# A hybrid decoder step: value products and query sums in fewer runs, products of the old states on GpSimd, small sample copies on ScalarE

## The chip, the cores and the metric

The kernel runs on one core of one Trainium2 chip. The metric is the device time of one execution in microseconds (us). Before the change, three runs took 1385.62, 1386.16 and 1386.54 us; the median is 1386.16. The engines are named as in the profile: PE is TensorE (matrix products; PEld its weight loads), DVE is VectorE, ACT is ScalarE, POOL is GpSimd, and SP issues most of the transfers.

## The reference

One layer of a hybrid decoder takes a prompt of 256 tokens and eight sample streams of one token each. The change touches the two mixers that run side by side: attention in a sliding window, and a state-space scan (SSD). What matters of the reference, cut:

```python
def swa_banded(q, k, v, sinks):          # prompt: chunks of 128, keys of the chunk and the one before
    logits = jnp.einsum('bnqkgd,bnskd->bnkgqs', qb, kk) * HEAD_DIM ** -0.5
    p = sink_softmax(logits, mask[None, :, None, None], sinks)
    o = jnp.einsum('bnkgqs,bnskd->bnqkgd', p, vv)
...
def ssd_scan(xs, dt, a, bm, cm, h0, chunk):
    la = jnp.cumsum(dt * a, axis=2)
    seg = la[:, :, :, None] - la[:, :, None, :]
    decay = jnp.exp(jnp.where(causal, seg, -jnp.inf))
    cb = jnp.einsum('bclgn,bcsgn->bclsg', cm, bm)
    y = jnp.einsum('bclsgh,bcsghp->bclghp', cb[..., None] * decay, xdt)
...
    y = y + jnp.einsum('bclgn,bcghpn->bclghp', cm, h_prev) * jnp.exp(la)[..., None]
...
def _layer(...):
    proj = rms_norm(x, w['g_mix']) @ w['w_in']
    q, k, v, z, xbc, dt_raw = jnp.split(proj, IN_SPLITS, axis=-1)
    q = rms_norm(q.reshape(b, t, N_HEADS, HEAD_DIM), w['q_norm_g'])
```

After that come the output projection, a cross-attention and a feed-forward part with a short convolution. For a sample token the scan has one step: its old state `h0` (32 heads of 64 by 128, for each of eight streams) is multiplied by C of that stream and summed over the 128 state entries; that is the product of the old states with C.

## The kernel before

Prompt and samples stand side by side as 264 columns. Every projection is cut into weight pieces of 128x1024 numbers. SP loads a piece into `wraw` (L83), ScalarE writes its high half `whi` (L89), VectorE the rest `wlo` (L90), each with four buffers. `mm3` makes three products of every 128x128 slice with the 264 columns: high by high (L104), high by low (L105), low by high (L106). A piece holds eight slices, so it feeds 24 products. `proj` runs them for a pair of output blocks and hands both to an `evac` function.

The order of the instructions on each engine isn't written by hand in the part that changes: the framework's scheduler builds it when the program is built, taking weights and evacuations first (`tc.high_priority`), and keeping each engine's program in that order. `tc.issue_after(x)` adds an order: what is written inside it stands behind x. Buffers and PSUM banks limit it too: there are three banks for "mm", two for "t", one each for "s", "x" and "y". So the small work of attention and scan stands between the large products of the input projection (to about 355 us of the span).

The small products use part of the array: a product with 64 output rows takes half of the columns, one with 32 rows a quarter, at an offset. Neighbouring products of that kind are called a run here.

- The log decays `la` are summed with the triangle `tri` (L479); L482 makes the same sums transposed, in 32 rows for each chunk, and `laT` goes to memory by SP for use in `ssd_prompt` (L810).
- `q_sums`: L620 sums the squares of the queries, eight products of 32 rows, for two halves d of four j.
- `attn_first(j)` handles the first chunk for j and j+1, `attn_prompt(j)` the second for one j: scores, softmax, four transposes (L283), a copy to `pt`, then four value products of 64 rows (L602 and L564), and a copy to `attn`.
- `conv_side` takes two convolution blocks: the evacuated `u` (a ring of four), a small copy of its sample columns to `cnew` (L746, 24 in all), and three steps on VectorE for each block (L750). `conv_sample` reads `cnew` (L757). `z_pair` makes the gates; L896 copies its sample columns to `zsam` (16).
- `ssd_prompt(g)` runs the scan for one group of heads; L830 has eight products of 64 rows a chunk; on GpSimd stand the sum of `xs` (L844) and the decay of `hp` (L851).
- `ssd_sample(g)` multiplies old states by C: GpSimd issues the loads of `cb` (one buffer, L870) and `h0` (three buffers, L873), VectorE multiplies 128x512 (L874) and sums (L875), 32 times.

Of the kernel before, what the change touches and what calls it, by code (L numbers as in the profile page):

```python
# [48 lines left out]
def hybrid_decoder_step_kernel(ctx: ExitStack, tc: tile.TileContext, I, O):  # L49
# [11 lines left out]
    def psum(tag):  # L61
        return ps.tile([128, 512], F32, tag=tag, name=tag, bufs=banks[tag])
# [415 lines left out]
    dtan2 = dtan.rearrange("p c h -> p (c h)")  # L478
    PE.matmul(p[:, 0:64], tri, dtan2, start=True, stop=True)  # L479
    PE.matmul(p[:, 64:128], ones, dtan2, start=True, stop=True)  # L480
    for c in range(2):
        PE.matmul(p[0:32, 128 + c * 128:256 + c * 128], dtan[:, c, :], tri, start=True, stop=True)  # L482
# [42 lines left out]
    def attn_prompt(j, rq, nrq, c):  # L525

        pp = j // 4
        nk = 128 * (c + 1)
# [39 lines left out]
    def attn_first(j):  # L568

# [26 lines left out]
            tr(p[:, i * 128:i * 128 + 128], e[:, i, :])  # L596
        pt = mp.tile([128, 4, 128], F32, tag="bc", name="pt", bufs=2)
        S.copy(out=pt, in_=p.rearrange("p (a q) -> p a q", q=128))
        o = psum("t")
        for i in range(4):  # L600
            h = i % 2
            PE.matmul(o[64 * h:64 * h + 64, 128 * (i // 2):128 * (i // 2) + 128], vn[:, 0, pp, 64 * h:64 * h + 64], pt[:, i, :], start=True, stop=True)  # L602
        S.copy(out=attn[:, j:j + 2, 0:128], in_=o[:, 0:256].rearrange("p (i q) -> p i q", i=2))


    qsq = [T3(apool, 4, tag="R", name=f"qsq{i}", bufs=4) for i in range(2)]
# [8 lines left out]

            S.activation(out=qsq[j // 4][:, j % 4, :TP], in_=qT[:, j, :TP], func=AF.Square)
    pq = psum("s")
    for d in range(2):
        for j in range(4):
            PE.matmul(pq[32 * j:32 * j + 32, 0:TP], nw[:, d, :], qsq[d][:, j, :TP], start=d == 0, stop=d == 1)  # L620
# [29 lines left out]
    def second_chunk(pp):  # L650
# [6 lines left out]
        for h, (hs, ho) in enumerate(halves):  # L657
# [2 lines left out]
            S.copy(out=hi, in_=x)  # L660
            V.tensor_tensor(out=qs[pp][ho, :, h, :], in0=x, in1=hi.bitcast(F32), op=ALU.subtract)

    for j in range(0, 8, 2):
        attn_first(j)
    for j in range(8):
        if j % 4 == 0:
            second_chunk(j // 4)
        d = 2 * (j // 4)
        attn_prompt(j, rqs[:, :, j % 4, d:d + 2], nrqs[:, :, j % 4, d:d + 2], 1)

    def attn_sample():

# [69 lines left out]
    def conv_side(b0, us, dst):  # L742
        c = mp.tile([128, 2, TP], F32, tag="c", name="c", bufs=2)
        for m, u in enumerate(us):
            bi = b0 + m
            V.tensor_copy(out=cnew[:, bi, :], in_=u[:, TP:])  # L746
            w = [cwh[:, i * 24 + bi:i * 24 + bi + 1] for i in range(4)]
            S.activation(out=c[:, m, :], in_=u[:, 0:TP], func=AF.Identity, scale=w[0], bias=cwh[:, 96 + bi:97 + bi])
            for i in range(1, 4):
                V.scalar_tensor_tensor(out=c[:, m, :], in0=u[:, i:i + TP], scalar=w[i], in1=c[:, m, :], op0=ALU.mult, op1=ALU.add)  # L750
        S.activation(out=dst, in_=c, func=AF.Tanh)
        V.scalar_tensor_tensor(out=dst, in0=dst, scalar=1.0, in1=c, op0=ALU.add, op1=ALU.mult)
# [113 lines left out]
    def ssd_sample(g):  # L866
        for q in range(2):
            rows = slice(4 * q, 4 * q + 4)
            cb = mp.tile([128, 4, 128], F32, tag="cb", name="cb", bufs=1)
            nc.gpsimd.dma_start(out=cb, in_=dram_bc[1][8 * g + 4 * q:8 * g + 4 * q + 4, :].partition_broadcast(128))  # L870
            for i in range(4):
                h0 = mp.tile([128, 4, 128], F32, tag="h0", name="h0", bufs=3)
                nc.gpsimd.dma_start(out=h0, in_=I["h0"][4 * g + i][:, rows, :])  # L873
                V.tensor_tensor(out=h0, in0=h0, in1=cb, op=ALU.mult)  # L874
                V.tensor_reduce(out=ych[:, 4 * g + i, rows], in_=h0, op=ALU.add, axis=AX.X)  # L875

    def conv_group(g):
# [711 lines left out]
```

## Time and profile before

| what | value |
|---|---|
| median of three runs | 1386.16 us |
| the profiled execution | 1386.54 us |
| its span | 1384.3 us |
| L90, `wlo` on DVE | 440 times, 540.7 us |
| L89, `whi` on ACT | 440 times, 459.5 us |
| L874, old states by C, DVE | 32 times, 22.5 us |
| L875, their sums, DVE | 32 times, 21.3 us |
| L746 and L896, small copies, DVE | 24 and 16 times, 3.9 and 2.4 us |
| L564 / L602, value products, records of PE | 64 / 32 |
| L620, query sums, records of PE | 16 |

A product in full precision leaves two records on PE, so a run of eight products shows 16. The span is what the profiler saw between the first and the last instruction; the time of an execution holds 2.24 us more in this one. In a row, a name such as `t<-xh,wlo` is the output tile and the inputs, and the bracket or the arrow behind an idle time names what ended it.

### The profile page before, as it was taken

Reading aid. Unit: us, or ns where it says so; the run is one execution under the profiler, and the core shown is the slowest. Engines: PE = TensorE matmul, PEld = TensorE weight load, DVE = VectorE, ACT = ScalarE, POOL = GpSimd, SP = SyncE. Lnnn points to the kernel's source line nnn. Section 1 sums busy time; section 2 is a strip of 40 time slices with the busy share of each in tenths; the row PEclk is TensorE's granted clock in tenths of the full one; section 3 lists DMA queues with packets and bytes.
Section 4 is the critical chain, followed back from the end, with each engine's and each line's share of the span. In section 5 each row is a group of like instructions: output and inputs, shape, how many; then the busy total and the mean of one; then the engine's idle time right before and its main releaser. Section 6 shows DMA issues by size and latency. Waiting matters only on the chain.

```text
span 1384.3 us, 28768 instructions
## 1 busy us (share of the span) xinstructions
PE 1376.5 (99%) x11415; PEld 1348.3 (97%) x11415; DVE 1048.7 (76%) x1865; ACT 766.1 (55%) x1261; POOL 94.8 (7%) x286
## 2 busy tenths in 40 slices
PE   9999999999999999999999999999999999999999
PEld 8999999999999999889999999999999999999998
DVE  7979799999987774478777775777577757765655
ACT  7667755556545555476565544554455445543532
POOL 0000011111000000002010000000000000000000
PEclk9999999999999999999999999999999999999999
DMA  7954467777677566766576765676667656655664
GB/s 296 331 163 135 145 209 254 232 245 259 234 220 239 182 240 211 308 219 193 187 256 216 259 210 188 214 255 214 186 214 244 196 185 198 198 183 185 192 188 139
DMA packets 89477, 298.31 MB, mean 215 GB/s; under 512 B 12032, under 2 KB 17152, under 8 KB 88832
## 3 DMA queue, kind: packets, MB, share of 16 engines
q1 hardware_dynamic: 83840, 277.61, 60.6%
q0 software_dynamic: 5504, 18.88, 4.2%
q8 instruction: 89, 1.46, 0.4%
q14 instruction: 44, 0.36, 0.1%
HBM read 280.77 MB, written 16.23 MB: 215 GB/s over the span
## 4 chain that ended last, share of the span: by engine, by line
PE 97%; DMA 1%; DVE 1%; ACT 0%; issue 0%; SPq 0%; ACTq 0%
PE mm L105 21%; PE mm L104 20%; PE mm L106 20%; PE t L105 10%; PE t L106 9%; PE t L104 9%; PE t L245 1%; PE t L283 1%; PE y L830 1%; DMA wraw<-in_w_co_dram 1%; PE y L846 0%; DMA open<-in_open_dram 0%; PE x L283 0%; DVE wlo L90 0%; PE s L245 0%; PE mm L245 0%
## 5 line engine op out<-in xcount | busy, mean ns | idle before, releaser
L89 ACT CAST whi<-wraw 128x1024 fp32r<-128x1024 f32 x440 | 459.5, 1047 | 518.2 <-PE mm L105 278.3
L90 DVE TENSOR_TENSOR wlo<-wraw,whi 128x1024 fp32r<-128x1024 f32 x440 | 540.7, 1231 | 220.8 <-ACT whi L89 214.9
L105 PE MATMUL t<-x2l,whi 128*128 128x264 f32 x704 | 200.6, 285 | 0.0
L105 PE MATMUL mm<-x2l,whi 128*128 128x264 f32 x704 | 200.5, 285 | 0.0
L105 PE MATMUL mm<-hl,whi 128*128 128x264 f32 x704 | 199.6, 285 | 0.0
L106 PE MATMUL t<-x2h,wlo 128*128 128x264 f32 x704 | 199.1, 283 | 0.0
L106 PE MATMUL mm<-x2h,wlo 128*128 128x264 f32 x704 | 198.7, 283 | 0.0
L106 PE MATMUL mm<-hh,wlo 128*128 128x264 f32 x704 | 197.6, 282 | 0.0
L104 PE MATMUL mm<-x2h,whi 128*128 128x264 f32 x704 | 196.5, 279 | 0.4 <-DVE res L1285 0.4
L104 PE MATMUL t<-x2h,whi 128*128 128x264 f32 x704 | 196.4, 279 | 0.0
L104 PE MATMUL mm<-hh,whi 128*128 128x264 f32 x704 | 194.1, 280 | 0.0
L104 PE MATMUL mm<-xh,whi 128*128 128x264 f32 x576 | 163.8, 286 | 0.0
L105 PE MATMUL mm<-xl,whi 128*128 128x264 f32 x576 | 163.5, 285 | 0.0
L106 PE MATMUL mm<-xh,wlo 128*128 128x264 f32 x576 | 162.1, 286 | 0.0
L104 PEld LDWEIGHTS mm<-x2h,whi 128*128 128x128 f32 x704 | 132.3, 188 | 0.6 <-ACT whi L89 0.6
L104 PEld LDWEIGHTS t<-x2h,whi 128*128 128x128 f32 x704 | 132.3, 188 | 0.0
L106 PEld LDWEIGHTS t<-x2h,wlo 128*128 128x128 f32 x704 | 132.1, 188 | 0.0
L106 PEld LDWEIGHTS mm<-x2h,wlo 128*128 128x128 f32 x704 | 132.1, 188 | 0.0
L106 PEld LDWEIGHTS mm<-hh,wlo 128*128 128x128 f32 x704 | 131.9, 188 | 0.0
L105 PEld LDWEIGHTS mm<-hl,whi 128*128 128x128 f32 x704 | 131.7, 187 | 0.0
L105 PEld LDWEIGHTS mm<-x2l,whi 128*128 128x128 f32 x704 | 131.7, 187 | 0.0
L105 PEld LDWEIGHTS t<-x2l,whi 128*128 128x128 f32 x704 | 131.7, 187 | 0.0
(497 smaller groups left out, 2893.8 us busy)
## 6 DMA issues: line engine op xcount, KB each, us to landing
wraw<-in_w_up_dram SPq DMA_DIRECT2D x176, 512.0 KB, 4.4
wraw<-in_w_in_dram SPq DMA_DIRECT2D x96, 512.0 KB, 4.7
wraw<-in_w_dn_dram SPq DMA_DIRECT2D x88, 512.0 KB, 4.4
wraw<-in_w_out_dram SPq DMA_DIRECT2D x48, 512.0 KB, 4.3
h<-in_h_dram POOLq DMA_DIRECT2D x32, 256.0 KB, 4.6
hn<-in_h_dram SPq DMA_DIRECT2D x16, 512.0 KB, 4.8
out_state_s_dram<-hn POOLq DMA_DIRECT2D x16, 512.0 KB, 3.6
e<-dram_la SPq DMA_DIRECT2D x16, 256.0 KB, 4.8
```

Of the source, the lines that this page charges most:

```text
L89: S.copy(out=hi, in_=x)
L90: V.tensor_tensor(out=lo, in0=x, in1=hi.bitcast(F32), op=ALU.subtract)
L104: PE.matmul(out, wh, xh, start=start, stop=False)
L105: PE.matmul(out, wh, xl, start=False, stop=False)
L106: return PE.matmul(out, wl, xh, start=False, stop=stop)
L245: PE.matmul(first[c][:, :T], pre[k // 2][i][:, k % 2, c * 128:(c + 1) * 128], A[k // 8][x][:, k % 8, :], start=k + i + x == 0, stop=k == K ...
L283: return PE.transpose(out, in_, cst[0:k, C_ID:C_ID + k])
L830: PE.matmul(y[o:o + 64, (h // 2) * 128:(h // 2) * 128 + 128], xdt[:, h, :], es[h // 4][:, h % 4, :], start=True, stop=True)
```

## The change

It has five parts. The transposed log decays are no longer summed by L482 but made by one transpose of `la` (64 rows, both chunks at once). The query sums begin with d=1, j=3, the last to be ready, and the other seven stand behind it by `issue_after`. The value products are taken out of the two attention functions, and two calls share one run of eight, which begins with the first product of the later call. The small copies of sample columns go from VectorE to ScalarE. The product of old states with C goes from VectorE to GpSimd, and its sum stays on VectorE.

```diff
-    for c in range(2):
-        PE.matmul(p[0:32, 128 + c * 128:256 + c * 128], dtan[:, c, :], tri, start=True, stop=True)
...
-    laT = next_u()[0:32, 3:259]
-    V.tensor_copy(out=laT, in_=p[0:32, 128:384])
-    nc.sync.dma_start(out=dram_la.rearrange("c h l -> h c l"), in_=laT.rearrange("p (c l) -> p c l", c=2))
+    laT = next_u()[0:64, 3:131]
+    p = psum("x")
+    tr(p[0:64, 0:128], la)
+    V.tensor_copy(out=laT, in_=p[0:64, 0:128])
+    nc.sync.dma_start(out=dram_la.rearrange("c h l -> (c h) l"), in_=laT)
...
-        pt = mp.tile([128, 4, 128], F32, tag="bc", name="pt", bufs=2)
+        pt = mp.tile([128, 4, 128], F32, tag=tag, name="pt", bufs=2 if tag == "bc" else 1)
         S.copy(out=pt[:, 0:2 * nb, :], in_=p[:, 0:2 * nk].rearrange("p (a q) -> p a q", q=128))
+        return pt
+
+    def second_values(j, pts):
+        pp = j // 4
         o = psum("t")
-        for h in range(2):
-            for kb in range(nb):
-                PE.matmul(o[64 * h:64 * h + 64, 0:128], vn[:, kb, pp, 64 * h:64 * h + 64], pt[:, h * nb + kb, :],
-                          start=kb == 0, stop=kb == nb - 1)
-        marks["attn"] = S.copy(out=attn[:, j, c * 128:c * 128 + 128], in_=o[:, 0:128])
+
+        def value(a, h, kb):
+            return PE.matmul(o[64 * h:64 * h + 64, 128 * a:128 * a + 128], vn[:, kb, pp, 64 * h:64 * h + 64], pts[a][:, 2 * h + kb, :],
+                             start=kb == 0, stop=kb == 1)
+
+        with tc.issue_after(value(1, 0, 0).ins):
+            for x in [(a, h, kb) for a in (1, 0) for h in range(2) for kb in range(2)][1:]:
+                value(*x)
+        marks["attn"] = S.copy(out=attn[:, j:j + 2, 128:TP], in_=o[:, 0:256].rearrange("p (i q) -> p i q", i=2))
...
+    def first_values(pp, pts):
...
+        with tc.issue_after(value(1, 0).ins):
+            for a, i in [(a, i) for a in (1, 0) for i in range(4)][1:]:
+                value(a, i)
+        S.copy(out=attn[:, 4 * pp:4 * pp + 4, 0:128], in_=o.rearrange("p (i q) -> p i q", i=4))
...
-    for d in range(2):
-        for j in range(4):
-            PE.matmul(pq[32 * j:32 * j + 32, 0:TP], nw[:, d, :], qsq[d][:, j, :TP], start=d == 0, stop=d == 1)
+    with tc.issue_after(q_sums(1, 3).ins):
+        for d in (1, 0):
+            for j in range(4):
+                if (d, j) != (1, 3):
+                    q_sums(d, j)
...
+    for pp in range(2):
+        first_values(pp, [attn_first(4 * pp + 2 * a) for a in range(2)])
...
+        second_values(j, [attn_prompt(x, rqs[:, :, x % 4, d:d + 2], nrqs[:, :, x % 4, d:d + 2], 1, tag)
+                          for x, tag in zip((j, j + 1), ("bc", "bc") if j % 4 == 0 else ("hp", "cb"))])
...
-            V.tensor_copy(out=cnew[:, bi, :], in_=u[:, TP:])
+            S.copy(out=cnew[:, bi, :], in_=u[:, TP:])
...
-                V.tensor_tensor(out=h0, in0=h0, in1=cb, op=ALU.mult)
+                P.tensor_tensor(out=h0, in0=h0, in1=cb, op=ALU.mult)
...
-            V.tensor_copy(out=zsam[:, 2 * i + m, :], in_=z[:, TP:])
+            S.copy(out=zsam[:, 2 * i + m, :], in_=z[:, TP:])
```

The lines of the changed program lie lower down: the query sums are L637, the second values L568, the first L615, the conv steps L774, the scan's products L854, the products of old states L898 and their sums L899.

Three places show how the order moves. The first is PE at the query sums, in the input projection. Before, the eight products stand in three runs:

```order
L106 MATMUL mm<-xh_77,wlo 128x264
L620 MATMUL s<-qsq_677,zz 32x256 x4
L620 MATMUL s<-qsq_678,zz 32x256 x2
L104 MATMUL mm<-xh_75,whi 128x264
...
L105 MATMUL mm<-xl_76,whi 128x264
L620 MATMUL s<-qsq_678,zz 32x256
L106 MATMUL mm<-xh_75,wlo 128x264
```

Now, with the transpose of `la` one large product ahead of them:

```order
L104 MATMUL mm<-xh_75,whi 128x264
L283 MATMUL x<-cst,la 64x128
L105 MATMUL mm<-xl_76,whi 128x264
L637 MATMUL s<-qsq_678,zz 32x256 x4
L637 MATMUL s<-qsq_677,zz 32x256 x4
L106 MATMUL mm<-xh_75,wlo 128x264
```

All eight stand together now, the half that is ready last first (`qsq_678`). The second place is PE at the value products of the second chunk (`vn` are the values). Before, four of them, next to transposes of the following probabilities `pe`:

```order
L106 MATMUL mm<-xh_77,wlo 128x264
L564 MATMUL t<-pt,vn 64x128 x4
L283 MATMUL t<-cst,pe 128x128 x4
L283 MATMUL x<-cst,bcs 32x128
L104 MATMUL mm<-xh_77,whi 128x264
```

Now:

```order
L105 MATMUL mm<-xl_78,whi 128x264
L106 MATMUL mm<-xh_77,wlo 128x264
L568 MATMUL t<-pt,vn 64x128 x8
L283 MATMUL x<-cst,bcs 32x128
L104 MATMUL mm<-xh_77,whi 128x264
```

The products of two calls stand in one run, and the transposes ahead of it. The third place is DVE at the second half of the old states of one group. Before, products and sums of `h` stand between the weight pieces and the scan:

```order
L90 TENSOR_TENSOR wlo<-wraw,whi 128x1024
L874 TENSOR_TENSOR h_3147<-h_3147,cb 128x512
L874 TENSOR_TENSOR h_3151<-h_3151,cb 128x512
L90 TENSOR_TENSOR wlo<-wraw,whi 128x1024
L739 TENSOR_TENSOR u_655<-mm,r_423 128x264
L752 SCALAR_TENSOR_TENSOR xs_2164<-xs_2164,c 128x2x256
L875 TENSOR_REDUCE ych<-h_3147 128x4
```

Now there are only the sums on DVE:

```order
L90 TENSOR_TENSOR wlo<-wraw,whi 128x1024
L899 TENSOR_REDUCE ych<-h_3135 128x4
L776 SCALAR_TENSOR_TENSOR xs_2152<-xs_2152,c 128x2x256
L899 TENSOR_REDUCE ych<-h_3139 128x4
L90 TENSOR_TENSOR wlo<-wraw,whi 128x1024
L899 TENSOR_REDUCE ych<-h_3143 128x4
```

The products of the same three tiles stand on POOL, between the issues of the loads:

```order
L894 DMA cb<-dram_bc 128x512
L897 DMA h_3143<-in_h_dram 128x512
L898 TENSOR_TENSOR h_3135<-h_3135,cb 128x512
L898 TENSOR_TENSOR h_3139<-h_3139,cb 128x512
L898 TENSOR_TENSOR h_3143<-h_3143,cb 128x512
L897 DMA h_3147<-in_h_dram 128x512
```

Each sum on DVE now stands behind a product on another engine, and the load of the next tile behind three products.

More of the change, by code (lines that the diff above doesn't have):

```diff
@@ L523, in hybrid_decoder_step_kernel, with attn_prompt @@
     V.tensor_scalar(out=nsink, in0=pc("sink_p", 0, 16), scalar1=-1.0, scalar2=None, op0=ALU.mult)
-    def attn_prompt(j, rq, nrq, c):
+    def attn_prompt(j, rq, nrq, c, tag):
         pp = j // 4
@@ L598, in attn_first, with value @@
         S.copy(out=pt, in_=p.rearrange("p (a q) -> p a q", q=128))
+        return pt
+    def first_values(pp, pts):
         o = psum("t")
-        for i in range(4):
+        def value(a, i):
             h = i % 2
-            PE.matmul(o[64 * h:64 * h + 64, 128 * (i // 2):128 * (i // 2) + 128], vn[:, 0, pp, 64 * h:64 * h + 64], pt[:, i, :], start=True, stop=True)
-        S.copy(out=attn[:, j:j + 2, 0:128], in_=o[:, 0:256].rearrange("p (i q) -> p i q", i=2))
+            c = 256 * a + 128 * (i // 2)
+            return PE.matmul(o[64 * h:64 * h + 64, c:c + 128], vn[:, 0, pp, 64 * h:64 * h + 64], pts[a][:, i, :], start=True, stop=True)
+        with tc.issue_after(value(1, 0).ins):
+            for a, i in [(a, i) for a in (1, 0) for i in range(4)][1:]:
+                value(a, i)
+        S.copy(out=attn[:, 4 * pp:4 * pp + 4, 0:128], in_=o.rearrange("p (i q) -> p i q", i=4))
     qsq = [T3(apool, 4, tag="R", name=f"qsq{i}", bufs=4) for i in range(2)]
@@ L617, in hybrid_decoder_step_kernel, with q_sums @@
     pq = psum("s")
-    for d in range(2):
-        for j in range(4):
-            PE.matmul(pq[32 * j:32 * j + 32, 0:TP], nw[:, d, :], qsq[d][:, j, :TP], start=d == 0, stop=d == 1)
+    def q_sums(d, j):
+        return PE.matmul(pq[32 * j:32 * j + 32, 0:TP], nw[:, d, :], qsq[d][:, j, :TP], start=d == 1, stop=d == 0)
+    with tc.issue_after(q_sums(1, 3).ins):
[3 more added lines that the diff above has]
+                    q_sums(d, j)
     cpc = mp.tile([128, 24, 8], F32, name="cpc")
@@ L661, in second_chunk @@
             V.tensor_tensor(out=qs[pp][ho, :, h, :], in0=x, in1=hi.bitcast(F32), op=ALU.subtract)
+    for pp in range(2):
+        first_values(pp, [attn_first(4 * pp + 2 * a) for a in range(2)])
     for j in range(0, 8, 2):
-        attn_first(j)
-    for j in range(8):
         if j % 4 == 0:
@@ L668, in hybrid_decoder_step_kernel @@
         d = 2 * (j // 4)
-        attn_prompt(j, rqs[:, :, j % 4, d:d + 2], nrqs[:, :, j % 4, d:d + 2], 1)
+        second_values(j, [attn_prompt(x, rqs[:, :, x % 4, d:d + 2], nrqs[:, :, x % 4, d:d + 2], 1, tag)
+                          for x, tag in zip((j, j + 1), ("bc", "bc") if j % 4 == 0 else ("hp", "cb"))])
     def attn_sample():
```

## The prediction

> **What bounds the kernel now.** I read the page first, from the top.
>
> ```profile
> span 1384.3 us, 28768 instructions
> PE 1376.5 (99%) x11415; PEld 1348.3 (97%) x11415; DVE 1048.7 (76%) x1865; ACT 766.1 (55%) x1261; POOL 94.8 (7%) x286
> PE 97%; DMA 1%; DVE 1%; ACT 0%; issue 0%; SPq 0%; ACTq 0%
> ```
>
> TensorE (PE) is busy for 99% of the span, and the third line, the chain that ended last, lies on it for 97%. So the time is the sum of what TensorE is given plus its few waits. The view of waits gives total, count and longest in us:
>
> ```profile
> PE x L206 <- DVE eps L279: 1.2, 1, 1.2
> ```
>
> That is the longest of six such rows with TensorE waiting, 4.4 us in all, and none between 31 and 580 us, where the change lies. A saving can come only from shorter work on TensorE, and a loss only from a wait that is new. What could be late is the low half of a weight piece, which VectorE (DVE) writes at L90. The next view has one stretch a row: its length, then busy us and count on PE, PEld, DVE, ACT and POOL, the granted clock, the DMA share and GB/s. The first two rows are of L90 alone, the next two of L106 alone, the last of everything.
>
> ```profile
> 0.00:185.30 185.30, 54.64 (x45) 1.00 0.62 209
> 0.00:294.10 294.10, 93.98 (x77) 1.00 0.68 222
> 0.00:191.40 191.40, 100.08 (x353) 65.91 (x353) 1.00 0.63 211
> 0.00:296.60 296.60, 170.14 (x609) 112.88 (x609) 1.00 0.68 222
> 185.30:294.10 108.80, 108.80 (x941) 105.71 (x940) 107.47 (x214) 60.72 (x103) 19.14 (x28) 1.00 0.77 242
> ```
>
> The 45th piece's low half is there at 185.3 us; L106 uses eight slices a piece, so its 353rd product, at 191.4, is the first that needs it: a lead of 6.1 us. The 77th is ready at 294.1 and needed at 296.6: 2.5 us. Between the two VectorE is busy for 107.5 of 108.8 us; it loses 3.6 us against TensorE. Here it is the second bound, close behind. The clock is 1.00 in all rows, so no term comes from it.
>
> **The change: TensorE.** A timeline row is the start, the duration, then engine, line, operation and count. Starts of the products after a run give its price.
>
> ```profile
> 355.80 0.28 PE L106 MATMUL t<-xh,wlo 128*128 128x264 f32 x1
> 355.92 0.28 PE L104 MATMUL t<-xh,whi 128*128 128x264 f32 x1
> 356.13 1.09 PE L830 MATMUL y<-e,xdt 128*64 128x128 f32 x16
> ...
> 357.38 0.28 PE L104 MATMUL t<-xh,whi 128*128 128x264 f32 x1
> 369.64 0.28 PE L105 MATMUL mm<-atl,whi 128*128 128x264 f32 x1
> 369.85 0.66 PE L830 MATMUL y<-e,xdt 128*64 128x128 f32 x8
> ...
> 370.67 0.28 PE L105 MATMUL t<-atl,whi 128*128 128x264 f32 x1
> ```
>
> A large product takes a slot of 0.12 us (355.80 to 355.92). The run of 16 records, eight products on half the columns, takes 1.46 from 355.92 to 357.38, less two slots 1.22. The run of 8 records takes 1.03, less two slots 0.79. So two runs of four products made into one of eight save 2 x 0.79 - 1.22 = 0.36: entering and leaving the column mode costs that much. The first values lose two runs (4 to 2, 0.72), the second ones four (8 to 4, 1.44; I take 1.4, since some stand beside transposes), and one run at L830 goes as the order falls (0.36): 2.5 us.
>
> ```profile
> 79.58 0.33 PE L479 MATMUL x<-dtan,cst 128*128 128x64 f32 x2
> 79.75 0.39 PE L480 MATMUL x<-dtan,cst 128*128 128x64 f32 x2
> 80.07 0.62 PE L482 MATMUL x<-cst,dtan 128*32 128x128 f32 x4
> ...
> 80.85 0.29 PE L106 MATMUL mm<-xh,wlo 128*128 128x264 f32 x1
> 81.22 0.28 PE L106 MATMUL mm<-xh,wlo 128*128 128x264 f32 x1
> 81.43 1.06 PE L620 MATMUL s<-qsq,zz 128*32 128x256 f32 x12
> 82.64 0.29 PE L105 MATMUL mm<-xl,whi 128*128 128x264 f32 x1
> 83.37 0.28 PE L105 MATMUL mm<-xl,whi 128*128 128x264 f32 x1
> 83.58 0.62 PE L620 MATMUL s<-qsq,zz 128*32 128x256 f32 x2
> ...
> 84.35 0.29 PE L104 MATMUL mm<-xh,whi 128*128 128x264 f32 x1
> ```
>
> Query sums: the run of 12 takes 1.42 less two slots, 1.18; that of 2 takes 0.98 less two, 0.74, and the third, alike, 0.74: 2.66 in all. One run of 16 lies above 1.18 and below 1.66, if the four added records cost no more than the 0.24 by pairs that starts at full width show; the middle, 1.42, saves 1.24 (1.0 to 1.48). Log decays: 79.75 to 80.85, 1.10, holds L480, the strip run and L105. Afterwards there is L480 at 0.17 (as from 79.58 to 79.75), one slot, and a transpose between one slot and 0.23: 0.41 to 0.52, so 0.6 is saved (0.58 to 0.69). Together 2.5 + 1.2 + 0.6 = **4.3 us** off TensorE (3.8 to 4.8). Nothing hides these: the chain runs through them.
>
> **The change: VectorE and GpSimd.** These rows group a line's instructions: count, busy us, mean ns, idle time before; the DVE rows between 185.3 and 294.1 us, the two POOL rows over the whole span. Then come timeline rows, the last from behind that stretch.
>
> ```profile
> L750 DVE SCALAR_TENSOR_TENSOR c<-u,par,c 128x256 f32<-128x256 f32 x38 | 18.7, 502 | 0.0
> L874 DVE TENSOR_TENSOR h<-h,cb 128x512 f32<-128x512 f32 x20 | 13.4, 681 | 0.9 <-DMA h<-in_h_dram 0.9
> L875 DVE TENSOR_REDUCE ych<-h 128x4 f32<-128x512 f32 x19 | 12.7, 676 | 0.0
> L746 DVE COPY cnew<-u 128x11 f32<-128x11 f32 x12 | 2.0, 164 | 0.0
> ...
> L844 POOL TENSOR_TENSOR xs<-xs,ti 128x512 f32<-128x512 f32 x4 | 9.1, 2264 | 2.5 <-DVE ti L843 2.4
> L851 POOL TENSOR_TENSOR hp<-hp,d 128x512 f32<-128x512 f32 x4 | 5.5, 1363 | 20.9 <-PE y L838 8.8 <-ACT xs L751 6.1 <-DMA wraw<-in_w_in_dram 5.9
> 239.83 1.04 POOL L851 TENSOR_TENSOR hp<-hp,d 128x512 f32<-128x512 f32 x1
> ...
> 240.26 1.69 DVE L90 TENSOR_TENSOR wlo<-wraw,whi 128x1024 fp32r<-128x1024 f32 x1 [0.32 <-ACT whi L89]
> ...
> 247.14 3.27 POOL L844 TENSOR_TENSOR xs<-xs,ti 128x512 f32<-128x512 f32 x1
> ...
> 249.20 1.50 DVE L750 SCALAR_TENSOR_TENSOR c<-u,par,c 128x256 f32<-128x256 f32 x1
> ...
> 290.39 1.31 POOL L851 TENSOR_TENSOR hp<-hp,d 128x512 f32<-128x512 f32 x1 [6.11 <-ACT xs L751]
> 290.72 1.26 DVE L875 TENSOR_REDUCE ych<-h 128x4 f32<-128x512 f32 x2
> 291.91 0.67 DVE L874 TENSOR_TENSOR h<-h,cb 128x512 f32<-128x512 f32 x1
> ...
> 342.00 2.37 DVE L874 TENSOR_TENSOR h<-h,cb 128x512 f32<-128x512 f32 x2
> ```
>
> A start-to-start distance for the 128x512 operations is 0.60 us (1.19 for the two reduces from 290.72 to 291.91). Between the 45th and the 77th low half VectorE now does 20 products (12.0 us) and 14 small copies (1.0 by the same distances, 0.075 each). Both go. But the order of the changed program has 30 reduces there for 19 (6.6 us more), and other work that it moves ahead, conv steps and parts of ssd_prompt, for 7.0 more. So the work in the stretch comes to 106.8 against 106.2 us by one set of prices: the relief is spent in the same stretch. TensorE's own share of moved small products makes its stretch longer too, 107.7 after 105.2 (191.4 to 296.6).
>
> What is new is contention. At 249.20 a conv step of mean 502 ns took 1.50 behind a GpSimd sum that ran from 247.14: about 1.0 us lost. The two reduces at 290.72 ran beside a GpSimd product at their usual 0.60. The products on GpSimd have no row; the nearest, L851 of the same size, takes 1.04 at best, against the 0.60 saved. I read the time lost on VectorE beside each of the eight GpSimd operations of ssd_prompt in that way (0.46 at 240.26, where L90 took 1.69 for its mean of 1.23; 1.09 at 342.00, where two products took 2.37 for 1.28): 0, 0, 0.19, 0.26, 0.31, 0.46, 1.02 and 1.09, 3.3 us beside 14.6 us of GpSimd (9.1 and 5.5), 0.23 a microsecond. A product of 1.04 at that rate costs 0.24. The changed order has more reduces near, and the share of VectorE's work with two operands in SBUF falls from about 66 to 57%, which makes x = **0.2 us** a product; the ends are 0 and 1.09.
>
> The first low half that VectorE can't give in time sets the stall. With 30 products and four operations of ssd_prompt in the stretch it is 34x + 0.9 (waits for DMA, as now) + 106.8 - 107.7 - 6.1 = **34x - 6.1**. At x = 0.2 that is 0.7 us.
>
> The Trainium skill ("SBUF — State Buffer", section "Who interferes with whom") speaks against this part: a VectorE instruction with two SBUF inputs and a GpSimd instruction that reads SBUF exclude each other for a whole instruction, while a reduce is never held. The trace agrees on the reduce (290.72) and on the one long hold (249.20); that two of eight operations cost nothing says that not every one meets such an instruction.
>
> The small copies on ScalarE cost nothing as long as it has room: it is busy for 60.7 of 108.8 us in the stretch, and 14 copies there would be 2.3 us at L746's 164 ns. If that cover goes, csm waits on VectorE for a copy, about 0.2 a block of four, eight blocks, 1.6 at most. On GpSimd's queue the products stand between the issues of the h0 and cb loads, so one that waits for its load or for cb holds the next load, and the hp and xs operations of ssd_prompt behind it; VectorE meets that only at L899 (rival 3). The pt copies that borrow the hp and cb buffers do so before the first cb load, which they could only delay. On SP's queue the write of la keeps its place, and one weight load now goes ahead of the first read of it, so no load comes later.
>
> **The sum.** The profiled execution took 1386.54, 2.24 outside the span; the sum is against the median, 1386.16, 0.38 below. 1386.16 - 4.3 + 0.7 = **1382.6**.
>
> **Rivals.** (1) *The holds eat the gain.* With x from 0.22 to 0.39 the stall is 1.4 to 7.2 us, and the net lies within about 0.2% (2.8 us, about what a measurement of this kernel can tell from no change). At x = 0.31 the stall is 4.4: 1386.3. For it: four of the eight values lie at 0.19 to 0.46. Against: those include operations longer than 1.04. Chance 0.26. (2) *The holds cost more than the runs save.* The place is the same stretch, the price x above 0.39; it ends slower. At the plain mean of the eight, 0.42, the stall is 8.2 and the time 1390.1; at 1.04 for each product, 29.3 and 1411. For it: two of eight reached 1.0, and VectorE hardly pauses, so a GpSimd operation nearly always meets something. Against: 18 us of reduces and the operations that read PSUM. Chance 0.21. By the skill's rule taken literally the 1411 would be the time. (3) *VectorE waits for GpSimd at the reduces.* L899 stands in VectorE's order; the next low half queues behind it. With 30 reduces each late by 0.3, on top of x = 0.2, the stall is 9.7: 1391.6. Chance 0.06; products are issued well ahead in the new order, with three buffers. (4) *The runs don't get cheaper*, since the value products of a pair now wait for the later pt on TensorE: 0.4 us at each of six runs takes 2.4 of the 4.3, which gives 1386.16 - 1.9 + 0.7 = 1385.0. No wait stands there now. Chance 0.05.
>
> **Numbers.** Faster 0.42 (the forecast), same 0.31 (1 and 4), slower 0.27 (2 and 3). The forecast's own range is 1381.0 to 1383.4. The whole range: below, 4.8 saved with no stall, 1381.4, and 0.4 for a sum read too small; above x = 0.53, stall 11.9, 1393.8, with the rest of the figures' rounding 1394.0. Higher x is left out, some 1 in 10.
>
> **What would show it.** Right: one run of 16 records at L637 of about 1.4 us, six value runs of 16 at 1.2, no TensorE wait for wlo between 185 and 310 us, conv steps with a mean near 0.5, L898 near 1.1. Wrong: rows "PE <- DVE wlo L90" in that stretch, L90 and L774 with means well above 1229 and 502 ns, or idle time of VectorE before L899 put down to GpSimd.

## The result and the profile after

The changed kernel takes 1401.56 us, the median of four runs (1400.66 to 1403.67), beside 1386.33 for the kernel before in the same comparison. The ratio is 1.0113, with a 95% interval of 1.0101 to 1.0125: 15.2 us slower. The forecast was 1382.6, with a range up to 1394.0.

The page of the changed kernel, its span, busy times and the chain that ended last:

```profile
span 1399.9 us, 28747 instructions
PE 1378.4 (98%) x11412; PEld 1350.8 (96%) x11412; DVE 1049.9 (75%) x1793; ACT 769.3 (55%) x1295; POOL 141.6 (10%) x318
PE 90%; DVE 3%; DMA 3%; POOL 2%; issue 1%; ACT 0%; SPq 0%; POOLq 0%; DVEq 0%
```

TensorE's idle time rose from 7.8 to 21.5 us, and its busy time from 1376.5 to 1378.4, although it has less to do. VectorE is as busy over the whole program as before (1049.9 for 1048.7): 32 products and 40 copies left it, and it has nothing to show for it. The waits of the changed kernel between 175 and 420 us (total, count, longest):

```profile
PE y L870 <- DVE ti L867: 3.9, 2, 3.5
DVE ych L899 <- POOL h L898: 3.5, 3, 2.2
PE mm L104 <- DVE u L763: 3.4, 2, 2.1
PE t L106 <- DVE wlo L90: 2.1, 2, 1.8
```

TensorE now waits for evacuations, for a low half and for parts of the scan, nearly all from VectorE (1.2 us are for ScalarE, in rows not shown), and VectorE waits for GpSimd at the sums. Groups of the same stretch show where VectorE's time went (count, busy us, mean ns, idle before):

```profile
L90 DVE TENSOR_TENSOR wlo<-wraw,whi 128x1024 fp32r<-128x1024 f32 x70 | 91.3, 1305 | 10.9 <-ACT whi L89 10.7
L774 DVE SCALAR_TENSOR_TENSOR c<-u,par,c 128x256 f32<-128x256 f32 x42 | 29.1, 710 | 0.0
L899 DVE TENSOR_REDUCE ych<-h 128x4 f32<-128x512 f32 x32 | 21.5, 673 | 3.5 <-POOL h L898 3.5
L898 POOL TENSOR_TENSOR h<-h,cb 128x512 f32<-128x512 f32 x32 | 51.1, 1603 | 45.5 <-DMA cb<-dram_bc 22.7 <-DMA h<-in_h_dram 22.5
```

A conv step costs 710 ns where it cost about 500, a weight piece 1305 where it cost 1229, and a sum what it always cost. On the timeline one sees it happen:

```profile
218.82 2.06 POOL L898 TENSOR_TENSOR h<-h,cb 128x512 f32<-128x512 f32 x1 [1.71 <-DMA h<-in_h_dram]
219.66 1.51 DVE L774 SCALAR_TENSOR_TENSOR c<-u,par,c 128x256 f32<-128x256 f32 x1
221.09 0.67 DVE L840 TENSOR_TENSOR e<-e,s 128x512 f32<-128x512 f32 x1
221.43 1.29 POOL L898 TENSOR_TENSOR h<-h,cb 128x512 f32<-128x512 f32 x1
221.69 1.09 DVE L785 SCALAR_TENSOR_TENSOR ysam<-tsm,csm 128x32 f32<-128x32 f32 x1
222.70 0.67 DVE L899 TENSOR_REDUCE ych<-h 128x4 f32<-128x512 f32 x1
```

The conv step at 219.66 has its two operands in SBUF and takes 1.51 beside the product at 218.82. L840, whose second operand is in PSUM, takes its usual 0.67 beside the next product. The tiny gate product at 221.69, with two operands in SBUF again, lasts until that GpSimd product is over. This is called a hold below. Its size for a whole kernel is the sum, over VectorE's instructions between 175 and 440 us, of what each takes beyond the usual duration of its form (the median over the kernel before and the one with the runs alone). In this kernel all instructions lengthened by more than 0.06 us stand beside GpSimd operations with two inputs.

### The profile page after: what moved, and what is told of

It reads as the page before. It is cut to its first block, busy times and chain, and to the rows that moved or that the text cites. A ratio compares the mean times of both kernels' runs of the same rounds, so it can differ in the third digit from the quotient of the medians.

```text
span 1399.9 us, 28747 instructions
## 1 busy us (share of the span) xinstructions
PE 1378.4 (98%) x11412; PEld 1350.8 (96%) x11412; DVE 1049.9 (75%) x1793; ACT 769.3 (55%) x1295; POOL 141.6 (10%) x318
## 4 chain that ended last, share of the span: by engine, by line
PE 90%; DVE 3%; DMA 3%; POOL 2%; issue 1%; ACT 0%; SPq 0%; POOLq 0%; DVEq 0%
PE mm L104 19%; PE mm L106 19%; PE mm L105 19%; PE t L104 9%; PE t L106 9%; PE t L105 9%; POOL h L898 1%; DMA h<-in_h_dram 1%; DMA cb<-dram_bc 1%; DVE c L774 1%; PE t L245 1%; DVE wlo L90 1%; PE t L283 1%; PE mm L245 0%; PE s L245 0%
## 5 line engine op out<-in xcount | busy, mean ns | idle before, releaser
L90 DVE TENSOR_TENSOR wlo<-wraw,whi 128x1024 fp32r<-128x1024 f32 x440 | 545.7, 1242 | 232.3 <-ACT whi L89 226.2
L106 PE MATMUL t<-x2h,wlo 128*128 128x264 f32 x704 | 198.5, 282 | 0.0
L106 PE MATMUL mm<-x2h,wlo 128*128 128x264 f32 x704 | 198.2, 282 | 0.0
L106 PE MATMUL mm<-hh,wlo 128*128 128x264 f32 x704 | 197.2, 282 | 0.0
L106 PE MATMUL mm<-xh,wlo 128*128 128x264 f32 x576 | 164.8, 288 | 0.0
L106 PEld LDWEIGHTS t<-x2h,wlo 128*128 128x128 f32 x704 | 131.9, 187 | 0.0
L106 PEld LDWEIGHTS mm<-x2h,wlo 128*128 128x128 f32 x704 | 131.8, 187 | 0.0
L106 PEld LDWEIGHTS mm<-hh,wlo 128*128 128x128 f32 x704 | 131.7, 187 | 0.0
```

Of the source, the lines that this page charges most:

```text
L90: V.tensor_tensor(out=lo, in0=x, in1=hi.bitcast(F32), op=ALU.subtract)
L106: return PE.matmul(out, wl, xh, start=False, stop=stop)
```

## The experiments

All times are medians. In the table, the 40th and the 110th piece are the starts of the first product (L106) with the low half of that weight piece, read from windows that count L106 (313 and 873 products); the holds are summed as said, with the number of GpSimd operations of two inputs in that stretch. Eight of those belong to the scan and are in every kernel. The runs of the kernel before beside these lie between 1386.0 and 1386.4.

| kernel | us | 40th piece | 110th piece | holds, us |
|---|---|---|---|---|
| before | 1386.2 | 175.3 | 404.8 | 3.3 of 8 |
| the change | 1401.6 | 171.4 | 420.7 | 24.1 of 40 |
| e1, products back on VectorE | 1385.2 | 171.8 | 404.0 | 4.6 of 8 |
| e2, runs alone | 1385.4 | 169.7 | 404.3 | 5.2 of 8 |
| e3, products on GpSimd alone | 1408.7 | 174.9 | 426.5 | 26.2 of 40 |
| e4, copies on ScalarE alone | 1391.7 | 174.6 | 410.2 | 6.7 of 8 |
| e5, zeros for products, cb unread | 1397.7 | 171.6 | 418.2 | 3.4 of 8 |
| e6, sum ahead of product | 1403.5 | 171.4 | 421.6 | 28.4 of 40 |
| f1, zeros for products, cb read | 1398.2 | 171.0 | 416.1 | 4.1 of 8 |
| f4, sum ahead, and zeros | 1394.4 | 170.5 | 412.2 | 4.4 of 8 |
| f6, one product in four on GpSimd | 1387.1 | 171.6 | 405.0 | 10.8 of 16 |
| f2, runs, no products | 1383.8 | 169.5 | 402.5 | 4.3 of 8 |
| f3, before, no products | 1387.2 | 174.5 | 404.7 | 6.2 of 8 |
| e9, half the sums on ScalarE | 1385.0 | 171.0 | 403.9 | 4.4 of 8 |
| f5, e9 with the copies on ScalarE | 1387.4 | 170.9 | 406.1 | 5.9 of 8 |
| e10, all sums on ScalarE | 1389.6 | 169.8 | 408.0 | 5.2 of 8 |
| g1, the change with tiles spread | 1393.4 | 171.1 | 411.4 | 22.2 of 40 |
| g2, g1 with products on VectorE | 1388.7 | 170.9 | 400.8 | 3.9 of 8 |

The framework orders each of these programs anew, so an edit is never alone: it also moves what stands around it.

### The parts of the change

In the changed kernel, e1 puts the products back; e2 also the small copies. In the kernel before, e3 moves only the products, e4 only the copies.

```diff
 e1  -                P.tensor_tensor(out=h0, in0=h0, in1=cb, op=ALU.mult)
     +                V.tensor_tensor(out=h0, in0=h0, in1=cb, op=ALU.mult)
 e2  as e1, and
     -            S.copy(out=cnew[:, bi, :], in_=u[:, TP:])
     +            V.tensor_copy(out=cnew[:, bi, :], in_=u[:, TP:])
     -            S.copy(out=zsam[:, 2 * i + m, :], in_=z[:, TP:])
     +            V.tensor_copy(out=zsam[:, 2 * i + m, :], in_=z[:, TP:])
 e3  the first edit the other way round, in the kernel before
 e4  the two others the other way round, in the kernel before
```

> The changed kernel with the products of old states back on VectorE (the other four parts stay). Holds theory (GpSimd's products hold VectorE's instructions with two SBUF operands, and VectorE was full): about 1382, that is 4.3 us under before, TensorE waits back to some 4.4 us and the clock at 1.00. Rival (the longer runs or the copies on ScalarE cause part of the loss): above 1386, with TensorE waits for attention or for csm still there.

> Only the runs and the transposed log decays are changed (parts 1 to 3); small copies and products stay on VectorE. Holds theory: 1381.9 (3.8 to 4.8 us under before). If the small copies on ScalarE matter, this differs from the kernel with them by more than 1 us; I expect less.

> The kernel before with only the products of old states moved to GpSimd. Holds theory: 1401 to 1406 (the loss of the whole change plus the 4.3 us that the runs saved), with conv steps near 0.72 us for 0.50. Rival (the loss needs the new order that the other parts make): below 1395.

> The kernel before with only the small sample copies moved to ScalarE. Expected within 1 us of before (1385.3 to 1387.3): 0.075 us a copy leaves VectorE and ScalarE has room. Rival (csm and the gates wait for ScalarE): 1 to 2 us slower.

e1 came to 1385.19 (ratio 0.9995, 0.9987 to 1.0004) and e2 to 1385.36 (0.9995, 0.9986 to 1.0004): the products cost the change 16.4 us, and the runs bring 1 us by the medians, which these intervals don't tell from nothing, where 4.3 were expected. e3 came to 1408.71, 22.5 us over before and more than expected, with conv steps at 641 ns. e4 was a miss: 1391.72, ratio 1.0042 (1.0028 to 1.0056).

What the runs do bring on TensorE is in the table: e2 reaches the 40th piece 5.6 us before the kernel before does, and the 110th 0.5 us before. Two windows of L106 alone, first of the kernel before, then of e2 (length, then busy us and count on PE, on PEld, clock):

```profile
0.00:404.86 404.86, 241.96 (x873) 160.79 (x873) 1.00 0.69 227
```

```profile
0.00:169.75 169.75, 88.92 (x313) 58.54 (x313) 1.00 0.65 221
0.00:404.35 404.35, 244.21 (x873) 160.99 (x873) 1.00 0.69 226
```

From the 35th to the 105th low half VectorE took 239.5 us before (11.7 idle) and 243.5 in e2 (15.2 idle). TensorE took 4.2 us longer over the same pieces, so it followed VectorE. Of e2's waits this one is new in size (0.9 before):

```profile
DVE h L898 <- DMA h<-in_h_dram: 6.1, 3, 3.8
```

In e4 VectorE waits 2.4 us for the first old state, the holds are twice those of before, and the lead of the 45th low half is 1.5 us for 6.1. So its loss too goes through VectorE in this stretch; why the order came out so was not isolated.

### Holds, or waits for GpSimd?

In the changed kernel e5 takes the holds away and leaves the waits, e6 takes the waits away and leaves the holds.

```diff
 e5  -                P.tensor_tensor(out=h0, in0=h0, in1=cb, op=ALU.mult)
     +                P.memset(h0, 0.0)
 e6  +                V.tensor_reduce(out=ych[:, 4 * g + i, rows], in_=h0, op=ALU.add, axis=AX.X)
                      P.tensor_tensor(out=h0, in0=h0, in1=cb, op=ALU.mult)
     -                V.tensor_reduce(out=ych[:, 4 * g + i, rows], in_=h0, op=ALU.add, axis=AX.X)
```

> The changed kernel, but GpSimd only fills each tile of old states with zeros in place of the product (the product with C is left out): the loads, the queue and the wait of each sum for GpSimd stay, and the GpSimd instruction no longer reads SBUF. Holds theory (VectorE's instructions with two SBUF operands wait while GpSimd reads): the lengthened instructions, 25 us in the changed kernel, fall to the few of ssd_prompt (3 to 7 us), and the time to 1383 to 1388. Rival (the sums wait in VectorE's order for a late GpSimd queue with one cb buffer): still above 1396.

> The changed kernel with each sum ahead of its product (so the sums are of the old states without C): GpSimd does as many products, but no instruction of VectorE waits for one. Holds theory: still 1396 to 1403, with lengthened instructions near 20 us or more. Rival (the sums wait for GpSimd): falls to 1390 or less.

e6 went as the holds theory has it: 1403.5, holds 28.4. e5 lost the holds, as expected, and was no faster for it, 1397.7. But nothing read cb any more, so its eight loads went one behind the other from 163 to 198 us, ahead of and among the first old states, and VectorE waited 18.6 us at the sums. f1 gives cb a reader again, and f4 does it with the sum ahead, so that neither hold nor wait for GpSimd is left:

```diff
 f1  -                P.tensor_tensor(out=h0, in0=h0, in1=cb, op=ALU.mult)
     +                P.memset(h0, 0.0)
     +                P.memset(h0, 0.0)
     +                P.tensor_copy(out=h0[:, 0, 0:8], in_=cb[:, 0, 0:8])
 f4  the same three lines behind the sum
```

> The changed kernel, but GpSimd fills each tile of old states twice with zeros and copies eight columns of cb into it (the product with C is left out): cb is read again, so its loads are paced as in the changed kernel, GpSimd is about as long busy, and it hardly reads SBUF. In the run with one fill and no reader of cb the holds were gone (3.4 us), but eight loads of cb stood one behind the other ahead of the old states. Holds theory: 1383 to 1390, waits of the sums for GpSimd below 5 us. Rival (GpSimd's queue is as much of a bound as the holds): above 1394, with over 10 us of VectorE waiting for GpSimd.

> The changed kernel with each sum ahead, and GpSimd filling the tile with zeros twice and copying eight columns of cb after it (the product with C is left out): neither holds nor waits of a sum for GpSimd, GpSimd as busy as with products. Two causes side by side: 1383 to 1388. Rival (a third cause, the order that draws all 32 sums ahead of the 77th weight piece): above 1393.

Both went as their rivals have it. f1: 1398.2, ratio 1.0083 (1.0069 to 1.0097). Its conv steps and its waits of the sums:

```profile
L901 DVE TENSOR_REDUCE ych<-h 128x4 f32<-128x512 f32 x32 | 21.6, 679 | 17.2 <-POOL h L900 17.0
L774 DVE SCALAR_TENSOR_TENSOR c<-u,par,c 128x256 f32<-128x256 f32 x42 | 21.1, 519 | 0.0
```

Twenty us of holds went, and 13.5 us more of waiting came (17.0 after 3.5). So the unread cb alone doesn't explain VectorE's waits in e5. The two don't add; the likely reading is that a VectorE that is held comes to its sum later and finds it ready, and one that isn't held comes early and waits. f4: 1394.4 (four runs from 1389.9 to 1397.4), with 12.5 us of waits at the sums, now for the loads themselves:

```profile
DVE ych L898 <- DMA h<-in_h_dram: 12.5, 8, 3.4
```

In neither e6 nor f4 does a sum wait for GpSimd, and their sums stand in nearly the same places; e6, with 28.4 us of holds, takes 9.1 us more than f4 with 4.4. But f4 is still 8.1 us over before, so there is a third cause. The order is part of it. Counted in low halves (L90) that stand ahead of them on VectorE, the first, 8th, 16th, 24th and 32nd sum of old states stand at (f2, further below, has neither the products nor the loads of cb):

```
before                       46  54  70  90 107
e1, products on VectorE      44  52  67  83  99
the change                   44  52  59  68  78
f4                           44  50  57  65  74
f2                           44  48  54  61  70
```

With 0.6 us a tile off VectorE, the scheduler draws all sums ahead. In the changed kernel the 32 sums start between 181.6 and 316.1 us, 4.3 us a tile. The order alone isn't the cause, as f2 shows: it draws its sums as far ahead, from 179.9 to 270.3 us, 2.9 us a tile, its VectorE waits 4.1 us for old states, and it takes 1383.8. What f4 has and f2 hasn't is the loads of cb and GpSimd's own work between the load issues (and the small copies on ScalarE); which of these makes the old states late was not separated. The chain that ended last in the changed kernel, from 190 to 330 us, lies for 42% on the products and the two kinds of load:

```profile
by line: POOL h L898 14.1%; DMA h<-in_h_dram 14.1%; DMA cb<-dram_bc 14.0%; DVE c L774 8.5%; issue 7.8%; DVE wlo L90 5.9%; PE t L105 3.7%; PE t L104 3.6%; PE t L106 3.5%; PE mm L104 2.9%; PE mm L106 2.8%; PE mm L105 2.8%; DVE ych L899 2.5%; 
```

On it a load takes 3.8 to 6.2 us, product and sum another 2, through three h0 buffers, and every fourth tile needs a new cb, which has one. GpSimd's own row above says the same: 45.5 us of idle ahead of L898, half for cb, half for h0.

### Whether it goes with the number of products

f6 leaves every fourth product on GpSimd (8 of 32).

```diff
-                P.tensor_tensor(out=h0, in0=h0, in1=cb, op=ALU.mult)
+                (P if i == 1 else V).tensor_tensor(out=h0, in0=h0, in1=cb, op=ALU.mult)
```

> The changed kernel with 8 of the 32 products on GpSimd and 24 on VectorE. If the cost goes with the number of products: 1388 to 1390 (1385.2 plus a quarter of 16). Rival (the queue and the drawn order cost only when all are there): 1384 to 1387.

1387.12, ratio 1.0011 (1.0001 to 1.002): 1.9 us over e1 for a quarter of the products, less than a quarter of 16.4. The holds do go with the number: 6.2 us more than e1 for 8 more operations, 0.78 each. That is more than the 0.60 that a product takes on VectorE. This one size lies between the two expectations and doesn't decide.

### The order spread

g1 keeps the products on GpSimd, but calls two tiles of old states after each pair of projections, from the second pair of conv_group(1) to the third of the output projection, each behind that pair's evacuation; g2 is the same with products on VectorE. The sums stand at the 51st to 106th low half in g1, at the 52nd to 114th in g2. (The expectations count a few pieces fewer, since they took a row of two for one.)

```diff
-    def ssd_sample(g):
...
+    def samples():
...
+                    with tc.issue_after(marks["ev"].ins):
+                        P.tensor_tensor(out=h0, in0=h0, in1=cb, op=ALU.mult)
+                        V.tensor_reduce(out=ych[:, 4 * g + i, rows], in_=h0, op=ALU.add, axis=AX.X)
+                    yield
...
+            if g > 1 or g == 1 and i == 2:
+                two_tiles()
```

> The changed kernel, products on GpSimd, but two tiles of old states after each pair of projections, so that the sums stand at the 48th to 99th weight piece of VectorE's order for the 42nd to 76th. If the drawn order turned the move into a loss (holds then only weigh as much as the products' time saved): 1385 to 1390. Rival (the holds alone carry the loss wherever the products stand): 1396 or more, with over 18 us of lengthened instructions and TensorE waits of over 8 us.

> The same spread order with the products on VectorE. If waits for old states' loads and VectorE's load at one place gave back the runs' saving: 1382 to 1384.5, under both kernels. Rival (VectorE's total work sets the time): 1385 to 1387.

g1 came to 1393.43 (ratio 1.006, 1.0046 to 1.0074), between the two expectations: half of the loss is gone, the holds are nearly all still there (22.2). g2 came to 1388.74 (1.0021, 1.0012 to 1.003), slower than e2 and outside both expectations. But up to the 110th piece it is what the runs promised:

```profile
0.00:170.95 170.95, 88.42 (x313) 58.45 (x313) 1.00 0.64 217
0.00:400.87 400.87, 244.47 (x873) 161.90 (x873) 1.00 0.70 229
```

It is 4.4 us ahead of the kernel before at the 40th piece and still 4.0 ahead at the 110th; TensorE has no wait in between. Then it loses 6.1 us around one wait (the 900th product of L106 stands 2.1 behind), since the last tiles stand too late for the sample gates; 4.5 are the wait, and for the 3.4 us behind it the granted clock is 0.50:

```profile
PE y L300 <- DVE accy L958: 4.5, 1, 4.5
```

In nearly the same spread order, the products on GpSimd put the 110th piece at 411.4 for 400.8: 10.6 us, with 22.2 us of holds for 3.9. At the end 4.7 us of that are left (g1 has no such wait at the gates).

### Less work on VectorE

e7 and e8 left the products out, with the runs and in the kernel before; f2 and f3 also leave out the loads of C for them.

```diff
 e7, e8  -                V.tensor_tensor(out=h0, in0=h0, in1=cb, op=ALU.mult)
 f2, f3  the same, and the tile cb and its load
```

> Only the runs and the transposed log decays are changed, and the products of old states with C are left out altogether (32 of 0.6 us less on VectorE). If VectorE's load from 175 to 390 us is what gave back the runs' saving, its relief lets it through: 1381.5 to 1382.5. Rival (the saving on TensorE is only about 1 us): 1385.

> The kernel before with the products of old states with C left out altogether. TensorE never waited in this stretch, so VectorE's relief should change nothing: 1385.5 to 1386.5; the distance to the same with the changed runs then is what the runs save by themselves, 3.8 to 4.8. Rival (VectorE's load costs time already before the change): 1384 or less.

> Only the runs and the log decays are changed; products of old states with C and the loads of C for them are left out (without a reader those loads had plugged GpSimd's queue, so that VectorE waited up to 7 us for old states). If VectorE's load is what gives back the runs' saving: 1381.5 to 1383. Rival (a wait of VectorE for the first old states in its order decides, whatever its load): 1385 or more, with such a wait of over 2 us.

> The kernel before without the products of old states and without the loads of C for them. TensorE never waited in this stretch before: 1385.5 to 1386.5. Its distance to the same with the changed runs is the runs' own worth. Rival as there: a wait of VectorE for old states of over 2 us, and 1388 or more.

e7 and e8 came to 1390.95 and 1397.51, both misses: the unread cb loads stood in the queue here too, and in e8 VectorE waited 7.0 us for one old state. Without these loads the times are 7.2 and 10.3 us shorter, though both a little over the ranges expected: f2 came to 1383.76 (ratio 0.9983, 0.9975 to 0.9992) and f3 to 1387.21 (1.0008, 0.9999 to 1.0017): with VectorE relieved of 19 us the runs are worth 3.4 us. e9, f5 and e10 try for that relief with nothing left out, by sums on ScalarE:

```diff
 e10 -                V.tensor_reduce(out=ych[:, 4 * g + i, rows], in_=h0, op=ALU.add, axis=AX.X)
     +                for b in range(4):
     +                    S.activation(out=h0[:, b, :], in_=h0[:, b, :], func=AF.Copy, accum_out=ych[:, 4 * g + i, 4 * q + b:4 * q + b + 1])
 e9  the same for odd i alone
 f5  e9 with the small copies on ScalarE
```

> The changed runs and log decays, copies and products on VectorE, and every second sum of old states on ScalarE (four instructions with an accumulator each, 16 of 32 sums, 9.5 us off VectorE). If VectorE's load in 175 to 390 us gave back the runs' saving: 1381.5 to 1383.5, under both kernels. Rival (ScalarE's whi pieces or evacuations come late for it): 1386 or more.

> Runs, log decays and small copies as in the change, products on VectorE, every second sum of old states on ScalarE: 11.6 us less on VectorE in all than in the kernel before. If VectorE's load gives back the runs' saving: 1382 to 1384. Rival (waits for old states' loads in VectorE's order do): 1385 to 1387.

> Runs and log decays as in the change, copies and products on VectorE, all sums of old states on ScalarE: 19 us off VectorE, some 40 us onto ScalarE. If VectorE's load gives back the runs' saving: 1382 to 1384. Rival (ScalarE now brings whi late): 1386 or more.

None came out as hoped: 1384.96 (0.9994, 0.9985 to 1.0003), 1387.39 (1.0006, 0.9997 to 1.0015) and 1389.64 (1.0024, 1.0014 to 1.0033). In e10 ScalarE is busy for 88.7 us from 185.3 to 294.1 (60.7 before), and VectorE waits 26.5 us for whi between 150 and 460. No version run here beats the kernel before by more than 0.1% and computes all of it.

## Why the prediction was wrong

**The bound was read right.** TensorE is the chain, VectorE stands close behind it from 185 to 300 us, and the loss came from new waits of TensorE for VectorE there, as the second rival had it.

**The size of x was the first step that failed.** It was taken as 0.2 us a product. The changed kernel has 24.1 us of holds beside 40 operations, 0.60 each; e3 gives 0.66, e6 0.71, g1 0.56. The eight values of the profile before, with a mean of 0.41, were turned down twice, once for the length of the operations and once for the share of reduces. Both were arguments, no measurements, and both went the wrong way: L898 took at least 1.27 us and 1.60 in the mean for the assumed 1.04 (the one at 218.82, begun while a weight piece ran on VectorE, took 2.06), and of the 32 instructions that were lengthened in the changed kernel 15 lost 0.9 to 1.1 us. With 0.60, 34x - 6.1 is 14.3, and the prediction's own sum 1396.2. That this comes near the result doesn't prove the formula: f1, with hardly a hold more than before, still takes 1398.2. The holds follow the rule that the prediction took from the Trainium skill ("SBUF — State Buffer", section "Who interferes with whom"): in these runs neither a sum nor an operation with an operand in PSUM was held, and zeros that GpSimd only writes held no operation with two operands. But not every GpSimd operation meets a victim, so the literal 1411 was too much. Counting operations with two operands alone also leaves some victims out. A small copy, with one operand, is held as well; here is one of e3, which takes 0.16 us undisturbed:

```profile
250.87 1.43 POOL L874 TENSOR_TENSOR h<-h,cb 128x512 f32<-128x512 f32 x1 [1.79 <-DMA h<-in_h_dram]
251.09 1.23 DVE L746 COPY cnew<-u 128x11 f32<-128x11 f32 x1
```

Six such copies make 5.2 of the 26.2 us of holds in e3. The change has them on ScalarE.

**What the formula had no term for** is the second step. The third rival, late products at the sums, got 0.06, since "products are issued well ahead in the new order". In the changed kernel only 3.5 us of it show, but in f1, without the holds, 17.0. The drawn order is the ground for it: it brings 32 tiles into a stretch in which the loads can't follow behind cb and GpSimd's own work (in f2, without both, they do), and spreading it (g1) takes 8.1 us of the 15.2 off. The prediction had counted the 11 additional sums in the stretch as VectorE's work, and not asked whether their tiles would be there. The chain of products, loads and sums through three buffers and one cb was named, and priced at nothing.

**The runs were priced right and booked wrong.** The forecast for them ahead of the 40th piece is 4.3 less 0.36 (L830 comes later), 3.9; the changed kernel stands at 171.4 for 175.3, 3.9 ahead. That the figures agree so well is in part luck, as the other kernels with these runs stand 3.5 to 5.8 us ahead there. The run of query sums shows the price itself:

```profile
84.34 0.37 PE L105 MATMUL mm<-xl,whi 128*128 128x264 f32 x1
84.64 1.07 PE L637 MATMUL s<-qsq,zz 128*32 128x256 f32 x16
...
85.87 0.28 PE L104 MATMUL mm<-xh,whi 128*128 128x264 f32 x1
```

From 84.34 to 85.87 are 1.53, less two slots 1.29, where 1.42 was taken. The third step that failed is "nothing hides these: the chain runs through them". It holds only up to the stretch in which VectorE sets the pace: e1 and e2 keep about 1 us, f2 against f3 3.4, and g2 4.0 up to the 110th piece. The profile before has the limit in it. The prediction read the lead of the low halves at the 45th and the 77th piece, 6.1 and 2.5 us, but between the two it is smaller. The 66th low half and the product that first needs it (the 521st of L106), in the kernel before:

```profile
0.00:259.95 259.95, 80.66 (x66) 1.00 0.66 217
0.00:261.15 261.15, 146.65 (x521) 96.94 (x521) 1.00 0.66 217
```

That is a lead of 1.2 us. As VectorE was full there and couldn't come sooner, a TensorE that comes 3.9 us sooner had to wait for all but some 1.2 of them, by this estimate; e1 and e2 kept 1.0 and 0.8.

**The copies** were priced at nothing. Within the changed order that holds (e1 against e2: 0.2 us), but alone they cost 5.5 us (e4) and beside half the sums on ScalarE 2.4 (f5 against e9), so the price seems to belong to the order they bring.

**The fourth rival** didn't come: no run of value products waits for a pt on TensorE.

**The clock** was left out with a reason that fell with the pauses. Windows of the changed kernel:

```profile
215.00:245.00 30.00, 24.82 (x188) 22.31 (x187) 27.69 (x48) 19.42 (x41) 17.15 (x20) 0.95 0.74 225
295.00:320.00 25.00, 23.40 (x184) 22.30 (x186) 25.00 (x48) 13.90 (x27) 10.05 (x7) 0.93 0.74 234
```

What stays open is how the loss splits: holds, waits for GpSimd and its loads, and drawn order cover one another, and taking away any one left 7 us or more over before. That the products' move costs 16.4 us is shown, and that each of the three is at work: 9.1 us between e6 and f4 for the holds, 10.6 between f4 and f2 for GpSimd's work and the loads of cb (with the small copies), 8.1 between the change and g1 for the order. These add up to more than the loss, so none of them is its share.

## What to carry to other kernels

Work that is moved off a full engine is only off it if the other engine neither holds it nor makes it wait: count what the two share, and what stands between them (buffers, queue, loads), before the durations. Where a second engine runs close behind the first over a long stretch, time saved ahead of that stretch is lent, not gained, until the second engine's work in it is less; read the smallest lead along the stretch, not only its ends. And where a scheduler sets the order, an edit is also a new order: compare where its neighbours stand, and whether their data can be there by then.

## What the runs showed of the hardware

After a pause TensorE ran slower for a while. In the changed kernel it waited 3.5 us up to 241.9; the products after that start 0.22 us apart, for 0.12 before:

```profile
238.16 0.28 PE L105 MATMUL mm<-xl,whi 128*128 128x264 f32 x1
241.92 1.90 PE L870 MATMUL y<-xw,Bn 128*128 128x512 f32 x2 [3.47 <-DVE ti L867]
242.82 1.21 PE L106 MATMUL mm<-xh,wlo 128*128 128x264 f32 x1
243.83 0.42 PE L104 MATMUL mm<-xh,whi 128*128 128x264 f32 x1
244.05 0.42 PE L105 MATMUL mm<-xl,whi 128*128 128x264 f32 x1
```

The granted clock was 0.50 from 242.1 to 245.5. It was 0.51 from 296.7 to 300.1 too, around waits of 1.9 us up to 291.5 and 1.6 up to 296.9, but stayed at 1.00 after waits of 2.1 up to 192.7 and 1.4 up to 205.9. So a wait on TensorE can cost more than its length, in the changed kernel some 3.4 us in all (half of the 6.8 at half clock, an estimate).

And 64 fills of 128x512 on GpSimd (33.8 us in f1) lengthened no operation of VectorE with two operands, while products of the same size did. Two of its small copies they did lengthen. Four copies that take 0.77 us together in the kernel before took 1.50 in f1, two of them lasting until a fill was over:

```profile
186.84 1.50 DVE L753 COPY attn<-tso 64x32 f32<-64x32 f32 x4
186.98 0.53 POOL L898 MEMSET h<- 128x512 f32 x1 [1.76 <-DMA h<-in_h_dram]
187.57 0.53 POOL L899 MEMSET h<- 128x512 f32 x1
```
